# HGRN2's features split at once into the place of the padded values, and the recurrence's gated input formed on VectorE, in a two-layer hybrid decoder on one core

## The chip, the core and the metric

The kernel runs on one core of one Trainium2 chip, as one launch. The metric is device microseconds (us) of that core, and fewer is better. Times given as the time of a kernel are medians of several runs; the profile is one further execution, with its own time. The engines are TensorE (PE in the rows, with its weight loads as PEld), VectorE (DVE), ScalarE (ACT), GpSimd (POOL) and SyncE (SP), which issues the transfers.

## What is computed

The reference is a trunk of two layers over one sequence of 512 tokens with 1024 features, all in float32. Each layer adds a mixer and then a feed-forward block to x, and a last norm follows:

```
h = rmsnorm(x, norm1_w[l]);  proj = h @ w_in[l]
lx, lg, rq, rk, rv, rg, hq, hf, hi, hg = split(proj)
y_lru = rglru(lx, lg, ...)       # conv of 4 taps, gates r and i, a = exp(-8 r softplus(-lam)),
                                 # u = sqrt(1 - a*a) * (i * xc), scan h = a*h + u, times gelu(lg)
y_ret = retention(rq, rk, rv, rg, ...)   # rotary q and k, decaying scores, head norm, times silu(rg)
y_hg  = hgrn2(hq, hf, hi, hg, lb[l], ...) # S = diag(f) S + (1-f) v^T, o = S^T silu(q), head norm, times silu(hg)
x = x + concat(y_lru, y_ret, y_hg) @ w_out[l]
x = x + conv_ffn(rmsnorm(x, norm2_w[l]))  # up, conv of 3 taps, silu(gate) * val, down
```

Retention and HGRN2 have four heads of 64 features (256 each for q, k or f, v and the gate), the recurrence (RG-LRU) has 512 features. The lower bounds `lb` come from a softmax over the layers of a small parameter.

## The kernel before, in words

Features lie on partitions, tokens along the free dimension: x is eight tiles of 128 x 512. To keep float32 precision with quick matmuls, every operand is split into two fp32r parts, a high one made by a copy on ScalarE and a low one made by a subtraction on VectorE (`xh`, `xl` of x or y, `wh`, `wl` of a weight, `gh`, `gl` of the feed-forward block). A product is then three matmuls (`mm3`, lines 320 to 324): high by high (L321), high by low (L322), low by high (L323). A norm's factor is not multiplied into x: x is scaled by the norm's weight when it is split, and the factor `rb` of each token is applied when a projection leaves PSUM.

Weights arrive in pieces of 128 x 1024 through three raw buffers, are split two pieces ahead of their use (`split_w`, `next_w`, lines 291 to 318) and lie in four pairs of buffers. PSUM's eight banks are four for large products (`mm`) and four for small ones (`sm`).

The order of every engine's instructions is written out at build time. `Flow` (lines 77 to 154) is a small planner: each chain of work is a generator, TensorE's main stream advances a clock by a fixed cost per product, and whenever the clock passes a chain's due time that chain emits its next operations. So each engine has one fixed queue, in the order in which the planner emitted them, and an instruction that waits holds up everything behind it on its engine. All operations of VectorE, ScalarE and GpSimd go through one helper, so that they all stand under line 185 in the rows, and small matmuls under line 327.

**The start** (`main` and `begin`, lines 1289 to 1373). ScalarE issues the load of the first norm's weights; SyncE loads x and the first two weight pieces in turn, in pieces of 256 KB. Nine warming matmuls run meanwhile. ScalarE and VectorE split x0, then half a weight piece in two steps, and so on. The first two output tiles share each piece of x (`joint`, line 499). The squares of x and their sum `ssq` come after all splits. `finish_norm` (line 419) takes the two first norms (one of each layer) through four small matmuls to `rms_ps`, a Newton iteration on 128 x 4 numbers, and four more matmuls that spread the factor to `rms_rps`; the second norms use `rsqrt_wide` (line 358), two wide matmuls with a matrix of ones and then Ln, Exp and Square on ScalarE. `setup_lb` (line 480) makes the lower bounds some 27 us into the run:

```
484  V.tensor_tensor(out=mx, in0=p0, in1=p1, op=ALU.max)
486  V.tensor_tensor(out=ex[:, 0, :], in0=p0, in1=mx, op=ALU.subtract)
487  V.tensor_tensor(out=ex[:, 1, :], in0=p1, in1=mx, op=ALU.subtract)
488  A.activation(out=ex, in_=ex, func=AF.Exp)
489  V.tensor_tensor(out=mx, in0=ex[:, 0, :], in1=ex[:, 1, :], op=ALU.add)
490  V.reciprocal(out=mx, in_=mx)
```

and seven more on VectorE up to line 497. `setup_small` (line 449) makes the constants `lamc` of the recurrence, with small operations on VectorE.

**The projections** (`mixers`, lines 1042 to 1067) take 28 tiles' worth of products in this order: hf0 hq0 hf1 hq1, hv, rq0 rk0, rv, rq1 rk1, lx0 to lx3, hg0 hg1 rg0 rg1, lg0 to lg3. A tile is eight products of 512 columns. The values hv and rv are wanted with tokens on partitions, so x is the stationary operand there and the weight moves, 256 columns at a time:

```
1049  banks.append(mm_ps.tile([128, 2, 256], F32, name="vps", tag="mm"))
...
1057  mm3(banks[c // 2][:, c % 2, :], n.h[kk][:, ts], n.lo[kk][:, ts], wh[:, sl], wl[:, sl],
1058      hf == 0 and k == 0 and c % 2 == 0, hf == 1 and k == 3 and c % 2 == 1, cost=0.374)
```

Four token blocks by eight pieces of x make 32 products for hv and 32 for rv. `evac_v` (line 555) applies the factor of each token on ScalarE. `hg_values` (line 704) copies hv into `vz`, a padded form in which each half of the tokens has zeros for the other.

Beside the main stream run the chains: HGRN2's (`hg_forget`, `hg_query`, then `hg_chain` with seven levels, each a group of small matmuls into one `sm` bank and a copy out of it), the two rotary and retention chains, and the recurrence (`lru_conv`, `lru_batch`, `lru_gate`). In `lru_batch` (line 899) GpSimd forms the gated input: `G.tensor_tensor(out=gts[j][1], in0=gts[j][1], in1=xcs[j], op=ALU.mult)`. GpSimd also makes the silu products of the gates (line 625).

Finished features are split into two parts by `split_y` (line 608) for W_out, in the order HGRN2, retention, recurrence (tiles 6, 7, 4, 5, 0 to 3). They take the places of `xh0`, `xl0` and so on, so each waits until the last projection has used that piece of x (`xfree`). W_out (`ops`) begins with two output tiles of six products each and then the missing two of each. The feed-forward block (`pps` for up, `dps` for down) follows; the last down projection of layer 0 adds to x (`add_x`), splits the new x for layer 1 and sums its squares, there on GpSimd (`square_x`, line 402). Layer 1 then starts with two tiles that use six pieces of x before they need the last two.

Of the kernel before, what the change touches and what calls it, by code (L numbers as in the profile page):

```python
# [15 lines left out]
S = 512  # L16
# [12 lines left out]


FIRST = ["x0", 0, "x1", 1, "x2", "x3", 2, "x4", "x5", 3, "x6", "x7"]
# [13 lines left out]
PL = _o  # L45
# [3 lines left out]
for _n, _w in (  # L49
# [9 lines left out]
WCOL = {"lx": 0, "lg": 512, "hg": 2816, "rg": 1792}  # L59
TAIL = "lx0 lx1 lx2 lx3 hg0 hg1 rg0 rg1 lg0 lg1 lg2 lg3".split()  # L60
TAIL = [(t[:2], int(t[2])) for t in TAIL]

WIN = (
    [("f", 2304), ("f", 2048), ("f", 2432), ("f", 2176), ("v", 2560, 0), ("v", 2560, 1)]
    + [("f", 1024), ("f", 1280), ("v", 1536, 0), ("v", 1536, 1), ("f", 1152), ("f", 1408)]
    + [("f", WCOL[n] + 128 * j) for n, j in TAIL]
)
WNAMES = (
    [("hf", 0), ("hq", 0), ("hf", 1), ("hq", 1), "hv", None]
    + [("rq", 0), ("rk", 0), "rv", None, ("rq", 1), ("rk", 1)]  # L70
    + TAIL
)
# [136 lines left out]
def kernel(ctx, tc, x_in, win, wout, wup, wdn, lruw, params, consts, out):  # L209
# [4 lines left out]
    low.tile([128, 896], F32, name="spare")  # L214
# [17 lines left out]
    csm = const.tile([128, CSMALL], F32, name="csm")  # L232
    cbig = const.tile([128, 2 * S], F32, name="cbig")
    msk = const.tile([128, len(LEVELS) - 1, 32], U8, name="msk")
    lamc = const.tile([128, DEPTH, 4, 3], F32, name="lamc")
    lbc = const.tile([128, DEPTH, 2, 2], F32, name="lbc")

    const.tile([128, 32], F32, name="pad")
    rpool.tile([128, 32], F32, name="pad")
# [22 lines left out]
    for l in range(DEPTH):  # L262
        wlist += [win[l, i] for i in range(len(WIN))]
# [94 lines left out]
    def rsqrt_wide(sq, r, tile_of, weights, name):  # L358


        h, lo = tile_of(F32R, 0), tile_of(F32R, 1)
        A.activation(out=h, in_=sq, func=AF.Copy)
        yield None
        V.tensor_tensor(out=lo, in0=sq, in1=h.bitcast(F32), op=ALU.subtract)
        yield None
        ps = yield from psum([128, S], name)
        small(0.216, out=ps, lhsT=weights, rhs=h, start=True, stop=False)
        small(0.216, out=ps, lhsT=weights, rhs=lo, start=False, stop=True)
# [16 lines left out]
    def new_norm(nw, pool):  # L385
        n = Norm()
        n.pool = pool
        n.nw, n.h, n.lo, n.sq, n.rb = nw, {}, {}, 0, None
        n.ssq = None
        n.fast = n.wide = False  # L390
        return n
# [27 lines left out]
    def finish_norm(n):  # L419
        if n.wide:  # L420

            v = rpool.tile([128, S], F32, name="rb")
            yield from rsqrt_wide(n.ssq, v, lambda t, i: rpool.tile([128, S], t, name="sq", bufs=3), ones, "rms_ps")
            n.rb = v
# [1078 lines left out]
```

## Time and profile before

| what | us |
|---|---|
| median of 3 runs | 1169.06 (1168.43 to 1169.92) |
| profiled execution, its own time | 1168.12 |
| its span, first to last instruction | 1166.3 |
| TensorE busy | 1154.9 (99%) |
| VectorE busy | 781.1 (67%) |
| ScalarE busy | 534.3 (46%) |
| GpSimd busy | 64.9 (6%) |
| layer 0: projections, from 5.25 on | to 176.9 |
| layer 0: W_out | 176.9 to 221.0 |
| layer 0: feed-forward | 221.0 to 580.5 |
| layer 1: projections | 580.5 to 750.3 |

Matmuls are pipelined: a matmul's row gives a duration longer than its share of TensorE, so a busy TensorE isn't one at its peak, and the distance between two starts is the better measure. A time in brackets behind a row is the idle time of that engine just before, and what ended it. A row with "x4" is four instructions merged.

### The profile page before, as it was taken

The page shows a single profiled execution, that of the slowest core. Times are in us where ns is not written, and L with a number is a line of the kernel's source. Part 1 is how long each engine was busy: PE and PEld are TensorE (multiplying, and loading weights), DVE is VectorE, ACT ScalarE, POOL GpSimd, SP SyncE. Part 2 cuts the span into 40 slices and gives each one's busy share as a digit, 9 for nine tenths or more (in the row PEclk, how much of TensorE's full clock was granted, in tenths as well). Part 3 has the DMA queues.
Part 4 walks back from the last instruction along what each step waited for, and adds up shares of the span by engine and source line. Part 5 has one row for each costly group of instructions (what it writes and reads, how often), then busy time and mean ns, then how long its engine had stood idle before and what let it go on. Part 6 is the DMA issues. An engine that isn't in the chain of part 4 may idle for free.

```text
span 1166.3 us, 15226 instructions
## 1 busy us (share of the span) xinstructions
PE 1154.9 (99%) x6046; PEld 961.6 (82%) x6046; DVE 781.1 (67%) x1162; ACT 534.3 (46%) x722; POOL 64.9 (6%) x51
## 2 busy tenths in 40 slices
PE   9999999999999999999999999999999999999997
PEld 7888778888888888888888877888888888888886
DVE  7887887577774575474668486955876646745645
ACT  6536874464443343232542568545444424433422
POOL 1011210000000000000310012100000000000001
PEclk9999999999999999999999999999999999999999
DMA  7232223223323332322432221423232232233222
GB/s 257 94 99 56 72 73 125 92 90 106 93 76 105 109 87 89 113 86 76 126 103 81 73 82 37 140 88 98 91 99 96 80 121 93 76 105 104 82 71 88
DMA packets 36455, 111.79 MB, mean 96 GB/s; under 512 B 4512, under 2 KB 5024, under 8 KB 36384
## 3 DMA queue, kind: packets, MB, share of 16 engines
q1 hardware_dynamic: 34560, 108.59, 29.6%
q10 hardware_dynamic: 1824, 2.23, 0.7%
q8 instruction: 47, 0.77, 0.3%
q14 instruction: 24, 0.20, 0.0%
HBM read 106.61 MB, written 2.10 MB: 93 GB/s over the span
## 4 chain that ended last, share of the span: by engine, by line
PE 96%; DVE 2%; DMA 1%; issue 0%; SPq 0%; ACT 0%; POOLq 0%; POOL 0%; DVEq 0%
PE pps L321 20%; PE pps L323 19%; PE pps L322 19%; PE dps L322 7%; PE dps L321 7%; PE dps L323 7%; PE ops L322 3%; PE ops L321 2%; PE ops L323 2%; PE vps L321 1%; PE vps L322 1%; PE vps L323 1%; PE k_o L327 1%; PE hg_pl L327 1%; PE lr_ps L327 1%; DVE qp L185 1%
## 5 line engine op out<-in xcount | busy, mean ns | idle before, releaser
L321 PE MATMUL pps<-xh,wh 128*128 128x512 f32 x1024 | 403.5, 394 | 0.0
L323 PE MATMUL pps<-xh,wl 128*128 128x512 f32 x1024 | 399.4, 390 | 1.3 <-DVE wl L185 1.3
L322 PE MATMUL pps<-xl,wh 128*128 128x512 f32 x1024 | 398.9, 390 | 0.0
L185 ACT ACTIVATE wh<-raw 128x1024 fp32r<-128x1024 f32 (+3 forms) x211 | 204.8, 973 | 150.5 <-PE dps L322 103.3
L185 DVE TENSOR_TENSOR wl<-raw,wh 128x1024 fp32r<-128x1024 f32 (+3 forms) x211 | 243.2, 1155 | 12.8 <-ACT wh L185 12.8
L321 PEld LDWEIGHTS pps<-xh,wh 128*128 128x128 f32 x1024 | 192.5, 188 | 43.2 <-issue 3.5
L323 PEld LDWEIGHTS pps<-xh,wl 128*128 128x128 f32 x1024 | 192.3, 188 | 42.5 <-DVE wl L185 2.1
L322 PEld LDWEIGHTS pps<-xl,wh 128*128 128x128 f32 x1024 | 192.6, 188 | 39.0 <-DVE xl L185 0.4
L185 DVE SCALAR_TENSOR_TENSOR hs<-pps,rb 128x512 f32<-128x512 f32 x88 | 60.4, 690 | 129.6 <-PE pps L323 129.6
L321 PE MATMUL dps<-gh,wh 128*128 128x512 f32 x320 | 124.5, 389 | 0.0
L322 PE MATMUL dps<-gl,wh 128*128 128x512 f32 x320 | 124.5, 389 | 0.0
L323 PE MATMUL dps<-gh,wl 128*128 128x512 f32 x320 | 124.5, 389 | 0.0
L185 DVE TENSOR_TENSOR x<-x,dps 128x512 f32<-128x512 f32 (+1 forms) x72 | 44.9, 627 | 107.4 <-PE dps L323 107.0
L185 ACT ACTIVATE cg<-hs,prm 128x512 f32<-128x512 f32 x44 | 35.9, 816 | 85.1 <-DVE hs L185 85.1
L185 ACT ACTIVATE cg<-cg 128x512 f32<-128x512 f32 x44 | 27.8, 632 | 93.9 <-DVE cg L185 93.9
L321 PEld LDWEIGHTS dps<-gh,wh 128*128 128x128 f32 x320 | 60.1, 188 | 12.6
L323 PEld LDWEIGHTS dps<-gh,wl 128*128 128x128 f32 x320 | 60.1, 188 | 12.4
L322 PEld LDWEIGHTS dps<-gl,wh 128*128 128x128 f32 x320 | 60.1, 188 | 12.4
L185 DVE SCALAR_TENSOR_TENSOR cvv<-hs,prm,cvv 128x511 f32<-128x511 f32 x88 | 65.9, 748 | 1.8
L185 DVE SCALAR_TENSOR_TENSOR cg<-hs,prm,cg 128x511 f32<-128x511 f32 x88 | 65.7, 747 | 1.5
L185 ACT ACTIVATE gh<-cvv 128x512 fp32r<-128x512 f32 x44 | 27.8, 631 | 73.6 <-DVE cvv L185 73.6
L322 PE MATMUL ops<-xl,wh 128*128 128x512 f32 x128 | 50.1, 391 | 0.0
(218 smaller groups left out, 1275.1 us busy)
## 6 DMA issues: line engine op xcount, KB each, us to landing
raw<-in_wup_dram SPq DMA_DIRECT2D x88, 512.0 KB, 3.5
raw<-in_win_dram SPq DMA_DIRECT2D x46, 512.0 KB, 3.5
raw<-in_wdn_dram SPq DMA_DIRECT2D x48, 384.0 KB, 3.0
raw<-in_wout_dram SPq DMA_DIRECT2D x16, 512.0 KB, 3.5
raw<-in_wdn_dram SPq DMA_DIRECT2D x16, 256.0 KB, 2.6
x<-in_x_dram SPq DMA_DIRECT2D x8, 256.0 KB, 5.3
sw<-ev ACTq DMA_DIRECT2D x32, 64.0 KB, 2.1
raw<-in_win_dram SPq DMA_DIRECT2D x4, 256.0 KB, 5.0
```

Source lines behind the costliest of these rows:

```text
L185: return fn(*args, **kw)
L321: T.matmul(out=ps, lhsT=ah, rhs=bh, start=start, stop=False)
L322: T.matmul(out=ps, lhsT=ah, rhs=bl, start=False, stop=False)
L323: T.matmul(out=ps, lhsT=al, rhs=bh, start=False, stop=stop)
L327: T.matmul(**kw)
```

## The change

The four HGRN2 tiles hf0, hf1, hq0, hq1 become one block in both layers: each piece of x meets all four before the next one, for six pieces, and each tile then takes its last two. hv and rv become one block of 32 products with 512 columns, two of its token blocks in `sm` banks. The values are no longer scaled: the token's factor goes into the keys instead, for HGRN2 by a product with three operands on VectorE, for retention by a squared factor. Both first norms use the wide form; the one of layer 0 (`whole`) as one plain fp32 matmul. `split_y` puts HGRN2's two features into the place of `vz` without a wait, and moves the other six two places forward. The recurrence's gated input moves from GpSimd to VectorE. At the start, x and weights alternate piece by piece, the weights are split 512 columns at a time, the squares are taken among the splits, and the lower bounds (`setup_lb`, with one more operation per layer) are made right behind the split of x0, from two small loads of their own on ScalarE's queue. `setup_small` runs for both layers at once, five operations on VectorE and the rest on GpSimd. The sums of squares for layer 1 move to VectorE. Leading blanks are shortened here.

```diff
+JOINT = [("hf", 0), ("hf", 1), ("hq", 0), ("hq", 1)]
+ALONE = "rq0 rk0 rq1 rk1 lx0 lx1 lx2 lx3 hg0 hg1 rg0 rg1 lg0 lg1 lg2 lg3".split()
...
-    small(0.216, out=ps, lhsT=weights, rhs=lo, start=False, stop=True)
+    if tile_of is None:
+        ps = yield from psum([128, S], name)
+        small(0.9, out=ps, lhsT=weights.bitcast(F32), rhs=sq)
...
+    v = rpool.tile([128, S], F32, name="rb")
+    parts = None if n.whole else lambda t, i: rpool.tile([128, S], t, name="sq", bufs=3)
+    yield from rsqrt_wide(n.ssq, v, parts, ones, "rms_ps")
+    n.rb = v
...
+        V.tensor_scalar(out=lbc[:, l, :, 2], in0=lbc[:, l, :, 0], scalar1=0.5, scalar2=-0.5,
+                        op0=ALU.mult, op1=ALU.add)
+    setup_done.add("lb")
+def joint_tiles(n, done):
+    ws, pss = [], []
+    order = [(k, p) for k in range(KD - 2) for p in range(4)] + [(k, p) for p in range(4) for k in (KD - 2, KD - 1)]
+    for k, p in order:
+        if k // 2 == len(ws):
+            w = yield from next_w()
+            ws.append(w)
+        if k == 0:
+            yield from mm.take()
+            pss.append(mm_ps.tile([128, S], F32, name="pps", tag="mm"))
+        if k not in n.lo:
+            yield lambda: k in n.lo
+        wh, wl = ws[k // 2]
+        o = k % 2 * 512 + p * 128
+        mm3(pss[p], wh[:, o:o + 128], wl[:, o:o + 128], n.h[k], n.lo[k], k == 0, k == KD - 1)
+        yield None
+        if k == KD - 1:
+            done(p, pss[p])
...
+    if key[0] == "rk" and not rb2:
+        rb2.append(low.tile([128, NC, 2, 64], F32, name="hc_x").rearrange("p c h n -> p (c h n)"))
+        A.activation(out=rb2[0], in_=n.rb, func=AF.Square, scale=0.5)
+        yield None
-    V.tensor_tensor(out=t, in0=ps_of.pop(key), in1=n.rb, op=ALU.mult)
+    if key[0] == "rk":
+        V.tensor_tensor(out=t, in0=ps_of.pop(key), in1=rb2[0], op=ALU.mult)
+    else:
+        V.scalar_tensor_tensor(out=t, in0=ps_of.pop(key), scalar=-0.5, in1=n.rb, op0=ALU.mult, op1=ALU.mult)
...
-def evac_v(key):
...
+def values():
+    vz = low.tile([128, NC, 2, 256], F32, name="vz")
+    for b in range(2):
+        G.memset(vz[64 - 64 * b:128 - 64 * b, :, b, :], 0.0)
+    v = mp.tile([128, NC, 512], F32, name="v")
+    for c in range(NC):
+        yield has_ps(("v", c))
+        A.activation(out=v[:, c, :], in_=ps_of.pop(("v", c)), func=AF.Copy)
+        drop(sm if c < 2 else mm)
+    for b in range(2):
+        bs = slice(64 * b, 64 * b + 64)
+        A.activation(out=vz[bs, :, b, :], in_=v[bs, :, 0:256], func=AF.Copy)
+    vv["h"], vv["r"], vv["z"] = v[:, :, 0:256], v[:, :, 256:512], vz
+    yield None
+    evt.add("hv")
+    evt.add("rv")
...
 def split_y(src, k):
     i = YORDER.index(k)
-    yield has(("xfree", i))
-    h = xwpool.tile([128, S], F32R, name=f"xh{i}")
-    lo = xwpool.tile([128, S], F32R, name=f"xl{i}")
+    if i < 2:
+        if not ys:
+            ys.append(low.tile([128, 4, S], F32R, name="vz"))
+        h, lo = ys[0][:, 2 * i, :], ys[0][:, 2 * i + 1, :]
+    else:
+        yield has(("xfree", i - 2))
+        h = xwpool.tile([128, S], F32R, name=f"xh{i - 2}")
+        lo = xwpool.tile([128, S], F32R, name=f"xl{i - 2}")
...
-    V.tensor_scalar(out=kt, in0=kt, scalar1=olb, scalar2=None, op0=ALU.mult)
+    V.scalar_tensor_tensor(out=kt, in0=kt, scalar=lbc[:, l, ft, 2:3], in1=n.rb, op0=ALU.mult, op1=ALU.mult)
...
-        G.tensor_tensor(out=gts[j][1], in0=gts[j][1], in1=xcs[j], op=ALU.mult)
+        yield None
+        V.tensor_tensor(out=gts[j][1], in0=gts[j][1], in1=xcs[j], op=ALU.mult)
...
+yield from joint_tiles(n, done)
+banks, ws = [], []
+for q, c in [(q, c) for h in range(2) for q in range(2) for c in (2 * h, 2 * h + 1)] + [
+        (q, c) for q in (2, 3) for c in range(NC)]:
+    if q == len(ws):
+        w = yield from next_w()
+        ws.append(w)
+    wh, wl = ws[q]
+    ts = slice(c * 128, (c + 1) * 128)
+    if q == 0:
+        sl, pool, tag = ((sm, sm_ps, "sm") if c < 2 else (mm, mm_ps, "mm"))
+        yield from sl.take()
+        banks.append(pool.tile([128, 512], F32, name="vps", tag=tag))
+    for k in (2 * q, 2 * q + 1):
+        sl = slice(k % 2 * 512, k % 2 * 512 + 512)
+        mm3(banks[c], n.h[k][:, ts], n.lo[k][:, ts], wh[:, sl], wl[:, sl], k == 0, k == KD - 1)
+        yield None
+    if q == 3:
+        ps_of["v", c] = banks[c]
...
+    for l in range(DEPTH):
+        o = l * PL + PCOLS["lb"]
+        nc.scalar.dma_start(out=lbp[:, l, :], in_=params[:, o:o + 2])
+    for i in range(3):
         raws[i] = rawp.tile([128, 1024], F32, name="raw")
...
+    def piece(k):
+        c = slice(k % 2 * 512, k % 2 * 512 + 512)
+        nc.sync.dma_start(out=raws[k // 2][:, c], in_=wlist[k // 2][:, c])
+        fl.load(128 * 4 * 512)
+    for k in range(KD):
+        nc.sync.dma_start(out=x[k], in_=x_in[:, k, :])
         fl.load(128 * 4 * S)
+        if k < 6:
+            piece(k)
...
+        for k in range(6):
+            tile_x(k)
+            if k == 0:
+                setup_lb()
+            tile_w(k)
+            if k == 1:
+                raws[3] = rawp.tile([128, 1024], F32, name="raw")
+                piece(6)
+                piece(7)
+                nc.sync.dma_start(out=csm, in_=consts[:, 0:CSMALL])
+                fl.load(128 * 4 * CSMALL)
+                nc.sync.dma_start(out=prm[:, 8:], in_=params[:, 8:])
+                fl.load(128 * 4 * (DEPTH * PL))
+            if k in (3, 5):
+                fetch()
+            if k > 1:
+                square(k - 2)
+        for k in (6, 7):
+            tile_x(k)
+            square(k - 2)
+        square(6)
+        last = square_x(n, 7)
+        next(last)
+        next(last)
+        tile_w(6)
+        tile_w(7)
+        fetch()
...
-        setup_lb()
-        V.tensor_copy(out=ones, in_=dmean.to_broadcast([128, 128]))
...
+        n.fast = True
```

## Rows read from the trace of the kernel before

**Rows 1.** page, part 4: the chain that ended last, by engine
```profile
PE 96%; DVE 2%; DMA 1%; issue 0%; SPq 0%; ACT 0%; POOLq 0%; POOL 0%; DVEq 0%
```

**Rows 2.** waits of TensorE: line waited for: us in total, times, longest
```profile
PE pps L323 <- DVE wl L185: 1.3, 2, 0.6
```

**Rows 3.** busy time by stretch, 200 to 560 us: length, busy, count, clock, DMA
```profile
200.00:560.00 360.00, 360.00 (x1590) 1.00 0.31 93
```

**Rows 4.** timeline of TensorE, 31 to 33 us: start, duration, engine, line, operation
```profile
30.95 0.28 PE L321 MATMUL vps<-wh,xh 128*128 128x256 f32 x1
...
32.98 0.28 PE L323 MATMUL vps<-wh,xl 128*128 128x256 f32 x1
```

**Rows 5.** timeline of TensorE around the first norm of layer 0
```profile
21.33 1.05 PE L327 MATMUL rms_ps<-csm,ssq 128*128 128x1 f32 x8 [0.57 <-DVE ssq L185]
22.25 0.48 PE L321 MATMUL pps<-xh,wh 128*128 128x512 f32 x1
...
25.86 1.16 PE L327 MATMUL rms_rps<-csm,rms_rc 128*128 128x128 f32 x8
26.77 0.48 PE L321 MATMUL pps<-xh,wh 128*128 128x512 f32 x1
```

**Rows 6.** timeline of ScalarE and VectorE at the start
```profile
4.17 0.72 ACT L185 ACTIVATE xh<-x,prm 128x512 fp32r<-128x512 f32 x1 [1.49 <-DMA prm<-in_params_dram]
...
4.93 0.75 DVE L185 SCALAR_TENSOR_TENSOR xl<-x,prm,xh 128x512 fp32r<-128x512 f32 x1 [3.91 <-ACT xh L185]
...
7.24 0.69 DVE L185 TENSOR_TENSOR wl<-raw,wh 128x512 fp32r<-128x512 f32 x1 [0.23 <-ACT wh L185]
...
15.81 5.47 DVE L185 TENSOR_TENSOR ssq<-ssq,sq 128x512 f32<-128x512 f32 x7
```

**Rows 7.** timeline of TensorE at the start of W_out, layer 0
```profile
176.89 0.39 PE L321 MATMUL ops<-xh,wh 128*128 128x512 f32 x1
177.23 0.50 PE L322 MATMUL ops<-xl,wh 128*128 128x512 f32 x1
```

**Rows 8.** timeline of GpSimd: one of four gated inputs
```profile
124.43 1.30 POOL L185 TENSOR_TENSOR lr_g<-lr_g,qp 128x512 f32<-128x512 f32 x1 [8.77 <-ACT lr_g L185]
```

**Rows 9.** timeline of VectorE and GpSimd in the tail of layer 0
```profile
154.39 0.69 DVE L185 TENSOR_TENSOR ev<-pps,rb 128x512 f32<-128x512 f32 x1 [4.45 <-PE pps L323]
155.00 3.60 DVE L185 SCALAR_TENSOR_TENSOR qp<-qp,lr_g 128x512 f32<-128x512 f32 x4
158.52 3.45 DVE L185 TENSOR_TENSOR wl<-raw,wh 128x1024 fp32r<-128x1024 f32 x2
...
156.31 3.44 POOL L185 TENSOR_TENSOR ev<-ev,sq 128x512 f32<-128x512 f32 x2 [10.58 <-ACT sq L185]
```

**Rows 10.** timeline of VectorE: first and last of the set-up's twelve
```profile
26.86 0.15 DVE L185 TENSOR_TENSOR sm_m<-prm 128x2 f32<-128x2 f32 x1
...
28.87 0.17 DVE L185 TENSOR_SCALAR lbc<-lbc 128x2 f32<-128x2 f32 x1
```

**Rows 11.** timeline of TensorE at the start
```profile
1.06 4.21 PE L1301 MATMUL warm_ps<-zero 128*128 128x128 f32 x18 [1.06 <-DVE eps L1298]
...
6.33 0.63 PE L323 MATMUL pps<-xh,wl 128*128 128x512 f32 x1
6.75 0.57 PE L321 MATMUL pps<-xh,wh 128*128 128x512 f32 x1
7.15 0.39 PE L322 MATMUL pps<-xl,wh 128*128 128x512 f32 x1
7.38 0.39 PE L323 MATMUL pps<-xh,wl 128*128 128x512 f32 x1
```

**Rows 12.** timeline of VectorE: the copy out of a level's bank
```profile
48.56 1.30 DVE L185 COPY_PREDICATED st<-msk,hg_pl 128x512 f32<-128x512 uint8 x1
```

**Rows 13.** timeline of VectorE and TensorE where layer 1 starts
```profile
581.04 0.68 DVE L185 TENSOR_TENSOR x<-x,dps 128x512 f32<-128x512 f32 x1
...
582.54 0.39 PE L321 MATMUL pps<-xh,wh 128*128 128x512 f32 x1
```

More of the change, by code (lines that the diff above doesn't have):

```diff
@@ L213 @@
     const = ctx.enter_context(tc.tile_pool(name="const", bufs=1))
-    low.tile([128, 896], F32, name="spare")
+    low.tile([128, 864], F32, name="spare")
     xpool = ctx.enter_context(tc.tile_pool(name="xp", bufs=1))
@@ L262 @@
     for l in range(DEPTH):
-        wlist += [win[l, i] for i in range(len(WIN))]
+        wlist += [win[l, i] for i in range(NWIN)]
         wlist += [wout[l, m] for m in range(KD)]
@@ L389, in new_norm @@
         n.ssq = None
-        n.fast = n.wide = False
+        n.fast = n.whole = False
         return n
@@ L480, in setup_lb @@
+        G.tensor_tensor(out=s, in0=s, in1=z, op=ALU.mult)
+        G.tensor_scalar(out=s, in0=s, scalar1=2.0, scalar2=None, op0=ALU.mult)
+        G.tensor_tensor(out=s, in0=s, in1=rl, op=ALU.add)
+        for i, f in enumerate((-8.0, -16.0, 8.0)):
+            G.tensor_scalar(out=lamc[:, :, :, i], in0=s, scalar1=f, scalar2=None, op0=ALU.mult)
+        yield None
+    setup_done = set()
     def setup_lb():
         tp = rpool
-        p0, p1 = pc(0, "lb", 0, 2), pc(1, "lb", 0, 2)
+        p0, p1 = lbp[:, 0, :], lbp[:, 1, :]
@@ L1069, in mixers, with done @@
+        def done(i, ps):
+            ps_of[ALONE[i]] = ps
+        yield from matmul_tiles(n, len(ALONE), done, freed=lambda k: evt.add(("xfree", k)))
         n2 = new_norm(lambda k: pc(l, "n2", k), None)
-        n2.wide = True
         n2.fast = True
@@ L1298, in main @@
         nc.vector.memset(eps, EPS)
+        nc.vector.memset(mean, 1.0 / D)
+        nc.vector.tensor_copy(out=ones, in_=mean.to_broadcast([128, 128]))
         zps = sm_ps.tile([128, 128], F32, name="warm_ps", tag="sm")
@@ L1343, in begin @@
-            for i in range(2):
-                raws.pop(i)
-                ready[i] = ws[i]
-                fetch()
-            for _ in prep():
-                pass
-            for k in range(KD):
-                if k < KD - 1:
-                    for _ in square_x(n, k):
-                        pass
-                else:
-                    last = square_x(n, k)
-                    next(last)
-                    next(last)
-            fl.free.update(A=17.5, V=18.0)
-            fl.now = 5.8
@@ L1359, in begin, with tile_x @@
-            fl.spawn(last, 13.8)
+            ws = [(wp.tile([128, 1024], F32R, name="wh"), wp.tile([128, 1024], F32R, name="wl")) for _ in range(4)]
+            def tile_x(k):
+                h = xwpool.tile([128, S], F32R, name=f"xh{k}")
+                lo = xwpool.tile([128, S], F32R, name=f"xl{k}")
+                A.activation(out=h, in_=x[k], func=AF.Copy, scale=n.nw(k))
+                V.scalar_tensor_tensor(out=lo, in0=x[k], scalar=n.nw(k), in1=h.bitcast(F32),
+                                       op0=ALU.mult, op1=ALU.subtract)
+                n.h[k], n.lo[k] = h, lo
@@ L1360, in begin @@
+            for k in (6, 7):
[8 more added lines that the diff above has]
+            fetch()
+            fl.free.update(A=19.5, V=21.6)
+            fl.now = 5.2
+            fl.spawn(last, 15.0)
             yield 15.5
```

279 lines of the change are left out of this document (80 added, 199 removed).

## The prediction

> **What bounds the kernel.** I read the page first, its chain of work that ended last: 96% of it is TensorE [rows 1]. So a part of the change is worth what it takes out of TensorE's own stream of matmuls, plus the stalls that it removes, minus the stalls that it adds; time of another engine counts only where TensorE waits for it. The view of TensorE's waits says how little that is now: the longest entry is 1.3 us, in two waits [rows 2]. Because matmuls are pipelined, I price one by the distance from its start to the next start. In the quiet stretch from 200 to 560 us 1590 matmuls fill 360 us, 0.2264 us each [rows 3]; nearly all are 512 columns wide. A product (three matmuls) is therefore 0.68 us. The threshold used for the chances is 0.2% (2.3 us), about what a measurement of this kernel can tell from no change.
>
> **Values with 512 columns.** Before, hv and rv are 64 products of 256 columns in each layer, 384 matmuls in both. In a quiet piece 17 steps take 32.98 - 30.95 = 2.03 us, 0.1194 us each [rows 4]: 45.9 us. After, one block has 32 products of 512 columns in each layer, 192 matmuls at 0.2264: 43.5 us. That is -2.4 us. The small matmuls in between stay the same in number, and so do the changeovers between wide and small.
>
> **The two first norms.** Before, each takes two groups of eight passes: 22.25 - 21.33 = 0.92 us and 26.77 - 25.86 = 0.91 us [rows 5], 1.83 us a layer. In layer 1 they become two wide fp32r matmuls with the ones matrix, 0.45 us by [rows 3]: -1.4 us. In layer 0 it is one plain fp32 matmul of 512 columns, a form that this trace does not have. Bounds: 0.45 us (two such fp32r matmuls) and 0.92 us (eight fp32 passes of 128 columns [rows 5]); fp32 makes two passes here for each 128 columns, so I take the upper: -0.9 us. The first norm's matmuls also made TensorE wait 0.57 us for the sum of squares [rows 5]. After, the squares are done among the splits and the matmul stands 22 products into the stream instead of 21. What VectorE has to do by then, from 4.93 us on, is 14 splits of 0.69 to 0.75 us [rows 6], seven sums in 5.47 us [rows 6] and the set-up of 2.5 us worked out below; overlapping a little, that ends near 22 us, and the matmul comes at 23 us or later. That wait goes: -0.6 us. What is late next is rb, at about 29 us, as now; four tiles and eight products of the values run without it, to beyond 31 us, so nobody waits. ScalarE's added Ln, Exp and Square lie in that cover; beyond it every microsecond by which rb is later would cost one.
>
> **HGRN2's features split at once.** At the start of W_out the second matmul begins 0.34 us after the first instead of 0.23 [rows 7], because VectorE makes the low parts just in time. Two of eight splits leave this crowded place, and no copy waits for the last projection to let go of xh0: -0.3 us for both layers.
>
> **The gated input on VectorE.** GpSimd's product takes 1.30 us, four in each layer [rows 8]; VectorE needs 0.6 to 0.7 for one of that size [rows 9]. But VectorE is not free while GpSimd works: under the two products at 156.31 us, four operations of the size that takes 0.61 to the next start (154.39 to 155.00) take 3.60 us [rows 9], 1.2 us lost under the first of them, and the split behind them shows as much under the second. So VectorE gains or loses at most half a microsecond on each, in a stretch where TensorE has no wait. I cost it at nothing; what hides it is the two weights split ahead. In the same way the two-input product for kt in place of one-input, the squared rb for rk, lamc on GpSimd and the sums of squares of layer 1 moved from GpSimd to VectorE move work between engines that TensorE doesn't wait for. The 0.65 us stalls in each layer's tail [rows 2] come from GpSimd's silu products [rows 9], which stay; I leave them, bounds -1.3 and +1.3 us.
>
> **The start pays.** The change puts the whole set-up of the lower bounds between the split of x0 and that of the first weight. On VectorE and ScalarE it is a chain: three small operations, ScalarE's Exp, then nine more, from 26.86 to 29.04 us [rows 10], 2.2 us in the trace, and two multiplications are added (0.2 to 0.4): 2.5 us. Before, VectorE is through with xl0 at about 5.6 us and the third matmul, which needs the first low part of a weight, starts at 6.33 [rows 6, 11]. After, the set-up runs from 5.6 to 8.1, the first low part (now 512 columns, 0.69 us [rows 6]) is there at 8.8, and the third matmul starts there: +2.5 us. Nothing covers this; TensorE has nothing else to do. The small loads that the set-up needs follow the load of the norm weights, which lets ScalarE start at 4.17 us; issued 0.4 and 0.8 us behind it, they are there by about 5.2, before 5.6. From then on four tiles share each pair of x and weight, so 2.7 us of matmuls meet some 2.1 us of VectorE (two splits and a sum): no later hunger.
>
> Then the clock. The eighteen warming passes take 4.21 us, 0.23 each, against the 0.11 of such passes later [rows 5]; the first wide matmuls start 0.42 and 0.40 apart, and from 7.15 on 0.23 [rows 11]. The slow steps are the level of 1.2 GHz, the quick ones that of 2.4. Before the rise TensorE had worked from 1.06 us on with hardly a pause. After the change it pauses from 5.3 to about 7 and again from 7.8 to 8.8 us, and no row shows what the clock makes of that. Bounds: it is at the high level when work resumes (then the two slow steps go, -0.35 us), or as much low time lies behind the last pause as lay ahead of the rise in this trace, 6 us, to 14.8 us (14 matmuls, 12 more than before, at 0.2 us more each: +2.4 us). The row speaks for a late rise rather than none, so I take a value in the upper half: low to about 13 us, ten matmuls, eight more than before, +1.6 us. The Trainium skill, TensorE: Matmul & The Clock Gate, "What's actually happening", says that the low clock is the default and that activity releases it; the trace agrees with its two levels (0.42 and 0.23 us for the same matmul). By that rule the pauses speak against this change and the sum stands as it is; without it the sum would be about 2 us lower.
>
> **Sum:** -2.4 - 1.4 - 0.9 - 0.6 - 0.3 + 2.5 + 1.6 = -1.5 us. The profiled execution took 1168.12 us around a span of 1166.3, which gives 1166.6; the median of the runs is 1169.06, 0.94 above it, so the forecast for a median is **1167.5 us**.
>
> **Rivals.**
> A: the start does not pay twice. If the clock rises at once, or the set-up's small operations hide behind loads, the sum is between -3.4 (the clock alone) and -5.6 us (both), 1163.5 to 1165.7 us. For it: half of the set-up's time is the distance between tiny operations; against it: each waits for the one before, and the split of the weight stands behind them on both engines. Chance 0.27.
> B: slower, by the HGRN2 chain. Two of the four small PSUM banks now hold value products for some 22 us, just while the seven levels of the chain want a bank each. If the levels can no longer overlap the copy out of the bank before, each is late by such a copy, 1.30 us [rows 12], 8 us or more in all, and the recurrence behind it brings its features late to W_out. VectorE waits 4.45 us for TensorE ahead of the tail [rows 9], so there is about that much slack; the rival decides from 4.5 us of delay on, and at 8 us costs 3.5 us in each layer: 1167.5 + 7 = 1174.5 us. Against it: a level needs the keys and queries updated by the one before, so two banks should do. Chance 0.12.
> C: the beginning of layer 1. Four tiles now want four free banks at once. The last x sum starts at 581.04 us and lasts 0.68, and the fourth tile would start at 582.54 [rows 13], 0.8 us later. The sums of squares, now on VectorE, may use that up and 0.5 to 1.5 us more: 1168 to 1169 us, no change that can be told. Chance 0.13.
>
> **The numbers.** The forecast has 0.48. Around it lie the unknown tail (1.3 either way) and the clock's upper bound (0.8), 1166.2 to 1169.6 with both on one side. A gives faster; the forecast's own case lies close to the line at 1166.7 and gives 0.18 faster, 0.28 same and 0.02 slower; C gives same; B slower. Faster 0.45, same 0.41, slower 0.14. The range leaves out B and what lies beyond the other cases: 1163.0 to 1169.8.
>
> **What would show it.** Right: 192 value matmuls of 512 columns about 0.227 us apart; one rms_ps in layer 0 without a wait; a wait of some microseconds on wl before the third wide matmul, which starts near 8.8 us; steps of 0.42 us behind it. W_out of layer 0 then starts about 1 us from where it stands now, and layer 1 is 2 to 3 us shorter. Wrong: the third matmul before 7.5 us or quick steps at once (A); a gap on ops or pps ahead of the recurrence's features (B); a wait on x at the start of layer 1 (C).

## The result, and the profile after

The changed kernel takes **1175.73 us** (median of 4 runs, 1174.54 to 1177.04) beside 1168.74 us for the kernel before (4 runs, 1167.90 to 1169.92): a ratio of 1.0059, 95% interval 1.0043 to 1.0075. So it is slower, where the forecast was 1167.5 us and its range ended at 1169.8. The profiled execution took 1174.81 us around a span of 1173.0, 6.7 us over that of before.

The chain of work that ended last, by engine, in the page of the changed kernel (its part 4), which answers to [rows 1]:

```profile
PE 94%; DVE 4%; issue 1%; DMA 0%; POOL 0%; ACTq 0%; POOLq 0%; ACT 0%; DVEq 0%
```

VectorE now has 4% of the chain in place of 2%. The view of TensorE's waits (us in total, times, longest) says where, and answers to [rows 2]:

```profile
PE ops L313 <- DVE xl L175: 4.0, 4, 2.0
PE pps L312 <- ACT wh L175: 2.0, 1, 2.0
PE pps L314 <- DVE wl L175: 1.9, 2, 1.4
```

Two of these were forecast, the 2.0 us on ACT wh and 0.5 of the 1.9 on wl: the start. The others were not: 4.0 us in W_out on the low parts of the mixed features (three of the four waits in layer 0, the fourth, 0.63 us, in layer 1), and a stall of 1.4 us in layer 1's tail, that is in the last projections ahead of W_out. By stage, from the first to the first (or last) matmul of each, in the profiles of five kernels (the last three are explained below):

| stage, us | before | changed | product on GpSimd, own step (e5) | three edits (e7) | as e7, but product on VectorE (e10) |
|---|---|---|---|---|---|
| to the first matmul of W_out, layer 0 | 176.89 | 177.78 | 177.51 | 173.71 | 173.91 |
| W_out of layer 0, first to last | 43.85 | 49.82 | 46.11 | 44.63 | 48.95 |
| on to the first of layer 1 | 359.75 | 359.78 | 359.77 | 359.77 | 359.77 |
| on to W_out of layer 1 | 169.77 | 168.46 | 166.78 | 166.77 | 166.77 |
| W_out of layer 1, first to last | 43.29 | 44.21 | 43.29 | 43.29 | 44.13 |
| on to the last matmul | 365.73 | 365.75 | 365.75 | 365.76 | 366.12 |

So 0.9 us are lost up to W_out (forecast: about 1), **6.0 in W_out of layer 0**, and of layer 1's gain of some 3 us 1.7 are given back in its tail and 0.9 in its W_out.

**The start** came as forecast. TensorE of the changed kernel, against [rows 11] (start, duration, engine, line, operation, idle time ahead and its releaser):

```profile
7.21 0.79 PE L312 MATMUL pps<-xh,wh 128*128 128x512 f32 x1 [1.96 <-ACT wh L175]
...
8.95 0.80 PE L314 MATMUL pps<-xh,wl 128*128 128x512 f32 x1 [0.52 <-DVE wl L175]
9.54 0.63 PE L312 MATMUL pps<-xh,wh 128*128 128x512 f32 x1
9.97 0.63 PE L313 MATMUL pps<-xl,wh 128*128 128x512 f32 x1
...
13.38 0.48 PE L312 MATMUL pps<-xh,wh 128*128 128x512 f32 x1
```

The third matmul starts at 8.95 us instead of 6.33, and nine steps of 0.43 us follow, up to 13.4 us. Such a step, from one start to the next at the level of 1.2 GHz, is called a low step below; at the level of 2.4 GHz the step is 0.23 us. **Values** and the **first norm** of layer 0, against [rows 4, 5]:

```profile
26.44 1.02 PE L318 MATMUL rms_ps<-ssq,ones 128*128 128x512 f32 x2
26.90 0.80 PE L312 MATMUL pps<-xh,wh 128*128 128x512 f32 x1
27.54 0.40 PE L313 MATMUL pps<-xl,wh 128*128 128x512 f32 x1
...
33.47 0.39 PE L312 MATMUL vps<-wh,xh 128*128 128x512 f32 x1
...
37.10 0.39 PE L313 MATMUL vps<-wl,xh 128*128 128x512 f32 x1
```

Sixteen steps of the values take 3.63 us, 0.227 each. The norm is two passes without a wait. **W_out of layer 0**, against [rows 7]:

```profile
178.01 0.39 PE L313 MATMUL ops<-vz,wh 128*128 128x512 f32 x1
179.09 0.50 PE L314 MATMUL ops<-vz,wl 128*128 128x512 f32 x1 [0.69 <-DVE wl L175]
...
182.54 0.49 PE L313 MATMUL ops<-xl,wh 128*128 128x512 f32 x1 [2.02 <-DVE xl L175]
...
184.34 0.79 PE L313 MATMUL ops<-xl,wh 128*128 128x512 f32 x1 [0.84 <-DVE xl L175]
184.94 0.63 PE L314 MATMUL ops<-xh,wl 128*128 128x512 f32 x1
185.36 0.63 PE L312 MATMUL ops<-xh,wh 128*128 128x512 f32 x1
...
187.82 0.50 PE L313 MATMUL ops<-xl,wh 128*128 128x512 f32 x1 [0.55 <-DVE xl L175]
```

HGRN2's features are there (`vz` without a wait); what TensorE waits for, but for 0.69 us on a weight, is retention's and the recurrence's. The four waits are 4.1 us, and behind the third one come four low steps. That retention is late is seen on ScalarE, first the kernel before, then the changed one:

```profile
134.71 0.61 ACT L185 ACTIVATE sq<-rt_on 128x512 f32<-128x512 f32 x1
...
145.29 0.73 ACT L185 ACTIVATE lr_a<-lr_g,lamc 128x512 f32<-128x512 f32 x1
```

```profile
145.89 0.73 ACT L175 ACTIVATE lr_a<-lr_g,lamc 128x512 f32<-128x512 f32 x1
...
153.21 0.72 ACT L175 ACTIVATE lr_g<-lr_g,lamc 128x512 f32<-128x512 f32 x1
...
157.25 0.62 ACT L175 ACTIVATE sq<-rt_on 128x512 f32<-128x512 f32 x1
```

The Square with which the head norm of retention's second output begins stood 10.6 us ahead of the recurrence's batch (twelve Exp and Tanh); now it stands behind it, 22.5 us later than before. What hangs on it falls on VectorE into a stretch in which VectorE is hardly ever idle (changed kernel):

```profile
163.99 0.17 DVE L175 TENSOR_SCALAR hc_v<-hn_ps 128x8 f32<-128x8 f32 x1 [1.29 <-PE hn_ps L318]
...
165.41 1.21 DVE L175 SCALAR_TENSOR_TENSOR hc_nt<-hc_nt,hc_v 128x8 f32<-128x8 f32 x1
...
167.25 0.69 DVE L175 SCALAR_TENSOR_TENSOR hc_x<-hc_nt,hc_rc 128x512 f32<-128x512 f32 x1
...
181.80 0.69 DVE L175 TENSOR_TENSOR xl<-rt_on,xh 128x512 fp32r<-128x512 f32 x1
```

From 163.99 to the end of `hc_x` that is nearly 4 us, with 1.3 us of waiting ahead of it; the first scan of the recurrence starts at 172.60 us where it started at 166.23, and the splits that W_out waits for come behind that. The scans alone don't explain the waits: with the product on GpSimd (e5) the first scan starts at 172.92 us, and W_out is 3.7 us shorter all the same.

### The profile page after: what moved, and what is told of

It reads as the page before. It is cut to its first block, busy times and chain, and to the rows that moved or that the text cites. A ratio compares the mean times of both kernels' runs of the same rounds, so it can differ in the third digit from the quotient of the medians.

```text
span 1173.0 us, 14752 instructions
## 1 busy us (share of the span) xinstructions
PE 1154.7 (98%) x5826; PEld 949.2 (81%) x5826; DVE 777.2 (66%) x1113; ACT 543.9 (46%) x727; POOL 45.6 (4%) x59
## 4 chain that ended last, share of the span: by engine, by line
PE 94%; DVE 4%; issue 1%; DMA 0%; POOL 0%; ACTq 0%; POOLq 0%; ACT 0%; DVEq 0%
PE pps L312 19%; PE pps L314 19%; PE pps L313 19%; PE dps L312 7%; PE dps L314 7%; PE dps L313 7%; PE ops L313 2%; PE ops L314 2%; PE ops L312 2%; PE vps L312 1%; PE k_o L318 1%; PE hg_pl L318 1%; PE vps L314 1%; PE vps L313 1%; DVE wl L175 1%; DVE lr_g L175 1%
## 5 line engine op out<-in xcount | busy, mean ns | idle before, releaser
L175 ACT ACTIVATE wh<-raw 128x1024 fp32r<-128x1024 f32 (+2 forms) x212 | 204.8, 968 | 141.0 <-PE dps L313 103.3
L175 DVE TENSOR_TENSOR wl<-raw,wh 128x1024 fp32r<-128x1024 f32 (+2 forms) x212 | 239.3, 1132 | 20.3 <-ACT wh L175 20.3
L175 ACT ACTIVATE cvv<-hs,prm 128x512 f32<-128x512 f32 x44 | 35.9, 816 | 30.0 <-DVE hs L175 30.0
```

The source lines that it names most:

```text
L175: return fn(*args, **kw)
```

## Experiments

Theory: the loss is one of order, retention's second chain and the recurrence's batch changing places in queues that are fixed at build time. Rivals: the late start pushes everything; the early splits crowd VectorE; the product on VectorE costs its own time.

Runs of the kernel before beside them have medians of 1168.36 to 1168.70 us.

| run | edit (to the changed kernel, unless said) | median, us (runs) | ratio to before (95%) |
|---|---|---|---|
| e1 | set-up late | 1174.09 (4) | 1.0046 (1.0031 to 1.0061) |
| e2 | product on GpSimd, one step | 1171.36 (5) | 1.0035 (1.0020 to 1.0049) |
| e3 | HGRN2's split late | 1177.40 (4) | 1.0078 (1.0063 to 1.0093) |
| e4 | e1 and e2 | 1168.96 (10) | 1.0005 (0.9995 to 1.0014) |
| e5 | product on GpSimd, step of its own | 1168.70 (10) | 1.0004 (0.9995 to 1.0014) |
| e6 | Square first | 1171.69 (5) | 1.0033 (1.0020 to 1.0046) |
| e7 | e5, Square first, set-up late | **1163.18** (4) | **0.9957** (0.9942 to 0.9971) |
| e8 | kernel before, product on VectorE | 1169.21 (10) | 1.0008 (0.9999 to 1.0018) |
| e9 | Square first, set-up late, product on VectorE 2 us later | 1165.17 (6) | 0.9967 (0.9955 to 0.9980) |
| e10 | Square first, set-up late | 1168.85 (10) | 1.0002 (0.9993 to 1.0011) |
| e11 | 36 warming passes | 1175.36 (4) | 1.0053 (1.0038 to 1.0068) |
| e12 | e7 with HGRN2's split late | 1164.09 (4) | 0.9961 (0.9946 to 0.9975) |

### The start: e1 and e11

```
             for k in range(6):
                 tile_x(k)
-                if k == 0:
-                    setup_lb()
                 tile_w(k)
+                if k == 5:
+                    setup_lb()
```

Expected of e1: 

> Edit: the set-up of the lower bounds stands behind the sixth tile of x and weights (where it no longer precedes the first weight), nothing else moves. Order theory (the loss is in W_out of layer 0, made by the new order of the mixers' work): the start comes back to that of before (third wide matmul near 6.4 us instead of 8.95, low clock ending near 7 us instead of 13.4, four tiles done near 30.0), W_out of layer 0 still lasts about 50 us (50.05 now, 44.08 before), total 3.5 to 4.5 us under the changed kernel: 1171 to 1172 us. Rival (start theory: the late start and the late rb push every chain behind, and so the features): W_out of layer 0 falls back to 44 to 46 us as well, total 8 to 10 us under: 1165.5 to 1167.5 us.

Measured: the third matmul starts at 6.47 us, and W_out of layer 0 at 174.35, 3.43 us earlier. That is the start's price, and about the sum of its parts: 2.48 us of set-up and nine low steps at 0.2 us, less a wait of 0.95 us for the sum of squares that comes back. But W_out's four waits are the same to 0.02 us (0.68, 2.03, 0.82, 0.55), so the start theory falls. The median falls by 1.6 us only and misses the order theory's 1171 to 1172 us. In the profiled execution (1174.55 us) the clock took the rest: sixteen steps of 0.43 us in W_out instead of four. Two stretches of W_out, changed kernel and then e1 (length, busy time and count of PE, PEld, DVE, ACT and POOL, granted clock, DMA share, GB/s):

```profile
180.00:184.00 4.00, 1.48 (x6) 0.56 (x4) 4.00 (x7) 1.42 (x2) 0.00 (x0) 1.00 0.66 174
184.00:188.00 4.00, 3.11 (x7) 2.00 (x8) 4.00 (x6) 1.31 (x3) 0.00 (x0) 0.57 0.41 138
```

```profile
180.00:184.00 4.00, 3.01 (x7) 1.82 (x6) 4.00 (x6) 1.79 (x4) 0.00 (x0) 0.52 0.43 111
184.00:188.00 4.00, 3.62 (x9) 2.86 (x10) 2.22 (x4) 0.63 (x1) 0.00 (x0) 0.50 0.66 243
```

Only the quickest run of e1, 1171.80 us, lies in the order theory's range.

```
-WARM = 9
+WARM = 18
```

Expected of e11: 

> Edit to the changed kernel: thirty-six warming passes in place of eighteen (they multiply zeros and are read by nobody), so that TensorE works through the set-up of the lower bounds. Pause theory (TensorE's pauses of 2.0 and 0.5 us bring the low clock until 13.4 us): the third wide matmul still starts near 8.95 us, but its successors stand 0.227 us apart instead of 0.427 within a microsecond or so; nine steps of 0.2 us go, vps starts 1.5 to 2 us earlier (33.47 now), total 1173.5 to 1175 us. Rival (the clock rises at a time of its own whatever TensorE did): steps of 0.427 to 13.4 us as now, vps at 33.3 to 33.6.

```profile
1.05 7.23 PE L1312 MATMUL warm_ps<-zero 128*128 128x128 f32 x36 [1.05 <-DVE mean L1308]
...
8.87 0.50 PE L314 MATMUL pps<-xh,wl 128*128 128x512 f32 x1
9.20 0.40 PE L312 MATMUL pps<-xh,wh 128*128 128x512 f32 x1
9.44 0.39 PE L313 MATMUL pps<-xl,wh 128*128 128x512 f32 x1
```

With TensorE kept at work the third matmul stands where it stood, and from 9.20 us on the steps are 0.23 us. The values start at 31.22 us instead of 33.47. So the low clock at the start came of the pauses. The Trainium skill, TensorE: Matmul & The Clock Gate, "What's actually happening", has the low clock as the default that activity lifts; this pair of traces agrees. In the time it hardly shows (1175.36, just above the range expected): as in e1, sixteen low steps in W_out took back what the start gave.

### The product's engine: e2, e5, e8

```
-                yield None
-                V.tensor_tensor(out=gts[j][1], in0=gts[j][1], in1=xcs[j], op=ALU.mult)
+                G.tensor_tensor(out=gts[j][1], in0=gts[j][1], in1=xcs[j], op=ALU.mult)
```

Expected of e2: 

> Edit: the recurrence's gated input is formed on GpSimd again, in one step with the product before it; all else as changed. Order theory: W_out of layer 0 shrinks from 50.05 to 44 to 46 us, since the recurrence's batch and the second retention's chain stand as in the kernel before; total 4 to 6 us under the changed kernel, 1170 to 1172 us, the start as late as now (third matmul near 8.95 us). Start theory: the features are late all the same, 1174.5 to 1177 us.

In e5 the `yield None`, that is the step of its own, stays. Expected: 

> Edit: the recurrence's gated input on GpSimd, but in the step of its own that the change gave it. Engine theory (the product's place on VectorE makes the difference): as with GpSimd in one step, W_out of layer 0 lasts 45 to 47 us (49.82 in the changed kernel's profile, 46.23 with GpSimd in one step), total 1170 to 1172 us. Step theory (the extra step shifts the order of what is issued, whichever engine does the product): W_out 49 to 51 us, total 1174 to 1177 us.

In e8 it is the kernel before that gets `yield None` and `V.`. Expected: 

> Edit to the kernel before, not the changed one: only the recurrence's gated input goes to VectorE, in a step of its own. Order theory (the product on VectorE costs only where the new order of projections has put retention's second chain behind the recurrence): within 0.2% of the kernel before, 1167.5 to 1170 us, W_out of layer 0 at 44 to 45 us. Rival (the product on VectorE costs by itself, as four steps of 0.6 us in a full engine): W_out 46 to 48 us, 1171 to 1174 us.

Measured: with GpSimd W_out of layer 0 lasts 46.23 us (e2) and 46.11 (e5). e2 takes 1171.36 us, 4.4 under the changed kernel; it keeps a tail stall of 1.46 us in layer 1, with eight low steps behind it. e5 has none and takes 1168.70, below the range expected and **7.0 us under the changed kernel by this one product**. In W_out the engine theory holds against the step theory; in layer 1's tail the step counts too, since it is all that e2 and e5 differ in. In the old order (e8) the same move costs 0.8 us, just within what can be told from nothing; W_out lasts 45.03 us there, with one wait of 1.44, less than the rival wanted. So neither the product on VectorE nor the new order costs 7 us alone; together they do. TensorE's longest wait in W_out of e5:

```profile
PE ops L313 <- DVE xl L175: 2.2, 1, 2.2
```

In layer 1 the product's engine, in a step of its own, changes the order on ScalarE. Changed kernel and then e5:

```profile
719.30 0.72 ACT L175 ACTIVATE lr_a<-lr_g,lamc 128x512 f32<-128x512 f32 x1
...
727.25 0.62 ACT L175 ACTIVATE sq<-rt_on 128x512 f32<-128x512 f32 x1
```

```profile
715.69 0.63 ACT L175 ACTIVATE sq<-rt_on 128x512 f32<-128x512 f32 x1 [1.68 <-DVE rt_on L175]
...
717.64 0.72 ACT L175 ACTIVATE lr_a<-lr_g,lamc 128x512 f32<-128x512 f32 x1
```

Counted from layer 1's first matmul (587.38 and 583.40 us), the last Sigmoid ends at 129.01 us in both and retention's output leaves PSUM at 131.56 and 131.57. Only the queue differs: the planner has the batch issued ahead of the Square in one and behind it in the other. The batch needs nothing of the product; the quicker product merely lets the batch be issued 2.3 us sooner, and the Square then waits for all twelve. Layer 1 up to its W_out is 1.7 us longer for it (168.46 against 166.77 us, and 166.77 again in e6 below, where the Square is held ahead of the batch).

In layer 0, where e5 wins 3.7 us in W_out, this order does not change. In e2 and e5 the Square stands behind the batch as in the changed kernel: 2.5 us sooner in e5 (154.79 us), and only 0.25 us sooner in e2, whose W_out is just as short. ScalarE of e2:

```profile
145.63 0.72 ACT L175 ACTIVATE lr_a<-lr_g,lamc 128x512 f32<-128x512 f32 x1
...
157.00 0.61 ACT L175 ACTIVATE sq<-rt_on 128x512 f32<-128x512 f32 x1
```

What differs there comes behind the Square. These are the small matmuls that sum it on TensorE, in e2 and then in the changed kernel:

```profile
159.46 0.95 PE L318 MATMUL hn_ps<-csm,sq 128*128 128x2 f32 x8
```

```profile
163.00 0.95 PE L318 MATMUL hn_ps<-csm,sq 128*128 128x2 f32 x8
```

They stand 3.5 us later in TensorE's queue. `hc_x` then ends at 167.95 us instead of 164.69 in e2 (163.87 in e5), and retention's second low part, which W_out needs, at 184.29 instead of 181.53 (181.96 in e5). Which choice of the planner puts them later was not traced, and no run moves these matmuls alone. W_out of layer 1 does not follow the Square either: it lasts 43.32 us in e2, where the Square stands behind the batch (721.81 and 712.91 us), and 44.21 in the changed kernel.

### The split: e3 and e12

```
-            if i < 2:
...
-                h, lo = ys[0][:, 2 * i, :], ys[0][:, 2 * i + 1, :]
-            else:
...
-                yield has(("xfree", i - 2))
...
+            yield has(("xfree", i))
+            h = xwpool.tile([128, S], F32R, name=f"xh{i}")
+            lo = xwpool.tile([128, S], F32R, name=f"xl{i}")
```

Expected of e3: 

> Edit: HGRN2's mixed features wait again for the projections to let go of the x tiles; all else as changed. Order theory (the gate and the projections' order, not this split, make the features late): W_out of layer 0 stays at 50 to 51.5 us, and a wait on the first of HGRN2's features is added; total 0 to 2 us over the changed kernel, 1175.5 to 1178 us. Rival (crowding theory: the four early splits stand in VectorE's and ScalarE's fullest stretch ahead of the second retention's norm and push it back): W_out falls to 45 to 47 us, total 1171 to 1173 us.

Expected of e12: 

> Edit to the kernel with the three edits that took 1163.18 us: HGRN2's mixed features wait again for the projections to let go of the x tiles, as in the kernel before. If the split in the place of the padded values is worth what the forecast gave it (0.3 us for both layers), 1163 to 1164 us, with a wait of 0.1 to 0.5 us at the start of W_out; if it is worth what undoing it cost in the changed kernel (1.7 us), 1164.5 to 1165.5 us, with a wait of some 2 us there.

Measured: e3 takes 1177.40 us, W_out 50.41 with a wait of 3.74 us on the first of HGRN2's features: crowding falls, the early split is no part of the loss. e12 falls between its two expectations: the wait in W_out is 1.22 us instead of 0.68, W_out lasts 0.2 us longer (44.81), and the medians stand 0.9 us apart with intervals that overlap. So where the other features are in time the split is worth 0.2 to 0.9 us, which can't be told from the forecast's 0.3.

### Both first edits: e4

Expected: 

> Both of the first two edits: the set-up behind the sixth tile, and the gated input on GpSimd. Order theory: the two add up, 3.5 to 4.5 us from the start and 4 to 6 us from W_out of layer 0: 1166 to 1168 us, and below the kernel before. Start theory: as with the late set-up alone, 1165.5 to 1167.5 us, and no different from that one.

Measured 1168.96 us, 2.4 us under e2 alone and above the 1166 to 1168 expected. W_out starts at 174.39, as expected, and lasts 46.25; e2's stall in the tail of layer 1 is still there (1.46 us), and in the profiled execution, the slowest of the ten (1171.61 us), thirteen low steps follow it.

### The order alone: e6, e7, e9, e10

```
             sq = mp.tile([128, S], F32, name="sq", bufs=2)
             A.activation(out=sq, in_=src, func=AF.Square)
+            evt.add(("rsq", key))
...
             yield has(("on", ("h", 1)))
+            yield has(("rsq", ("r", 1)))
             for j in js:
                 r = gts[j][0]
```

Expected of e6: 

> Edit to the changed kernel: the recurrence's batch of twelve Exp and Tanh waits until the Square of retention's second output has been issued; the gate stays on VectorE. Late-norm theory (that Square stands behind the batch, at 157.25 us instead of 134.71, so its eleven small steps, 2.3 us, and their neighbours fall into the stretch in which VectorE is never idle, from 157 us on): the Square comes near 150 us, the small steps before 158, and although the batch is some 4 us later, TensorE's idle time in W_out of layer 0 falls from 4.1 us to 2 to 3, total 1172.5 to 1174.5 us. Rival (the recurrence's own chain is the bound): the batch is late by 4 us and W_out waits 4 us longer, total 1178 to 1180 us.

Measured 1171.69 us, **4.0 us under the changed kernel with the same operations on the same engines**. The Square stands at 149.78 us, the small steps end by 157, and the batch, 5.8 us later than in the changed kernel, harms less than expected: waits of 3.2 us in W_out, none in layer 1's tail. The total beat the expected range, the waits stayed above theirs. By stage the two profiles differ by 2.6 us: layer 1 up to its W_out is 1.7 us shorter and W_out of layer 0 1.2 (48.65), while 0.3 are lost at the start. W_out of layer 1 stays long (44.14).

Expected of e7 (e5's engine, e6's order, e1's set-up): 

> Three edits to the changed kernel: set-up behind the sixth tile, gated input on GpSimd in a step of its own, Square of retention's second output ahead of the recurrence's batch. If the losses are the start (3.4 us) and the features late at W_out of layer 0 (4.1 us of idle time and what the clock adds), both go: third wide matmul near 6.4 us, idle time in W_out at most 1 us, total 1164 to 1167 us, under the kernel before by 2 to 4 us. Rival (the loss moves to another wait, as in the tail of layer 1): 1168 to 1170 us.

```profile
PE ops L313 <- DVE xl L175: 0.7, 1, 0.7
PE rms_ps L318 <- DVE ssq L175: 0.7, 1, 0.7
```

Measured 1163.18 us, a little under the range expected and 5.2 us under the kernel before: it beats both. Its large products have no stretch of low steps.

In e9 the product stays on VectorE but is issued 2 us later; e10 is its control.

```
-                yield None
+                yield 2.0
                 V.tensor_tensor(out=gts[j][1], in0=gts[j][1], in1=xcs[j], op=ALU.mult)
```

Expected of e9: 

> Edits: set-up behind the sixth tile, Square of retention's second output ahead of the recurrence's batch, and the gated input on VectorE but issued 2 us later in the order, so that VectorE's queue need not stand on it until ScalarE's Sigmoid is through (1.58 us of idle time ahead of the third one in layer 0). Queue theory (VectorE may do the product for nothing if it is issued when its input is there): no idle time on VectorE ahead of lr_g, idle time of TensorE in W_out of layer 0 at most 1 us, total as with GpSimd, 1162.5 to 1164.5 us. Rival (four products of 0.6 us on VectorE cost by themselves): W_out idle 2 to 3 us, 1166 to 1168.5 us, as with the product issued at once.

Expected of e10: 

> The control for the run before: the same but for the 2 us, the product on VectorE issued at once. Queue theory: idle time of 1.5 us on VectorE ahead of the third lr_g in layer 0, TensorE's idle time in W_out of layer 0 about 3 us as with the Square first alone (3.16), total 3 to 4 us under that run's 1171.7: 1167.5 to 1169 us. Rival (with the start gone the place no longer matters): within 1 us of the run before.

Measured 1165.17 us, between the ranges of the two theories, and 1168.85, as expected: 3.7 us by the place of four products in a queue. But not for the reason given. VectorE's third product, in e9 and then in e10:

```profile
130.23 0.69 DVE L175 TENSOR_TENSOR lr_g<-lr_g,qp 128x512 f32<-128x512 f32 x1 [4.11 <-ACT lr_g L175]
```

```profile
130.87 0.69 DVE L175 TENSOR_TENSOR lr_g<-lr_g,qp 128x512 f32<-128x512 f32 x1 [1.58 <-ACT lr_g L175]
```

VectorE idles longer ahead of it in the better kernel, so that wait is not what counts, and the queue theory as I had put it falls. The difference shows in W_out, e9 and then e10:

```profile
176.97 0.69 DVE L175 TENSOR_TENSOR xl<-lr_g,xh 128x512 fp32r<-128x512 f32 x1
...
178.78 0.68 DVE L175 TENSOR_TENSOR xl<-lr_g,xh 128x512 fp32r<-128x512 f32 x1
179.38 2.35 DVE L175 TENSOR_TENSOR wl<-raw,wh 128x1024 fp32r<-128x1024 f32 x2
```

```profile
177.84 0.68 DVE L175 TENSOR_TENSOR xl<-lr_g,xh 128x512 fp32r<-128x512 f32 x1
178.45 2.35 DVE L175 TENSOR_TENSOR wl<-raw,wh 128x1024 fp32r<-128x1024 f32 x2
180.72 0.69 DVE L175 TENSOR_TENSOR xl<-lr_g,xh 128x512 fp32r<-128x512 f32 x1
```

In e9 two of the recurrence's low parts pass ahead of two weight splits (2.35 us), in e10 one does, and TensorE waits 1.91 us for the second, with low steps behind. Which chain the planner serves first there follows from the product's place 45 us earlier; the path from one to the other was not traced step by step. Between e9 and e7 2.0 us are left; how much of them is the four products' own time on VectorE, and how much is order, isn't shown.

e10 and e7 differ in the product's engine alone, with the Square ahead of the batch in both: **5.7 us** (1168.85 against 1163.18), by stage 4.3 in W_out of layer 0 and 0.8 in that of layer 1. So holding that one order leaves most of what the product's move costs.

## Why the prediction was wrong

**The step that failed is "The gated input on VectorE": "I cost it at nothing; what hides it is the two weights split ahead".** It weighed durations (0.7 us against 1.3, and the time that GpSimd's product takes from VectorE) and found them even. With the rest of the change held fixed the move costs 7.0 us (e5), and 5.7 with the set-up late and the Square held ahead of the batch (e10 against e7). Most of it lies in W_out of layer 0 (3.7 and 4.3 us). The operation's chain shares every queue with other chains, and its move changed places in them. In layer 1 the batch, which takes ScalarE for 8 us, passes ahead of retention's Square, 1.7 us. In W_out of layer 0 the low parts come later, without a change of place between Square and batch; there the same four products on the same engine, issued 2 us later, win back 3.6 us (e9 against e10). I named who waits for the product, not who is overtaken. By which choices of the planner the product's place reaches W_out some 45 us later stays open. "Values with 512 columns" failed beside it: it counted the matmuls and left out what the new order does to the other chains. With both value blocks ahead of retention's first query the query leaves PSUM at 68.87 us instead of 54.60, and retention's second output at 148.69 instead of 133.32, behind the start of the batch instead of ahead of it. That puts the Square behind the batch in layer 0, with the product on either engine; holding it ahead wins 4.0 us in the changed kernel (e6). No run changes the order of the projections alone, so its share, also in the 2.3 us that W_out of e5 still lasts longer than before, is argued from these rows and not shown.

**Most of the rest of the sum held.** Set-up +2.5: 2.48 (e1). Clock +1.6: nine low steps where the sum had ten; two stand there before, so seven are added, 1.4 us, and e11 shows that they go when the pauses are filled. Values -2.4: 192 matmuls at 0.227. Norms: layer 0's two fp32 passes take 0.46 us and the matmul behind them 0.64 instead of 0.23, 0.87 in all, near the upper bound (0.92) that I took for the kind of matmul; layer 1's stretch up to W_out is 3.0 us shorter in e5 and e7, 0.65 of it the old tail stall; the 2.35 left stand against 2.75 in the sum for that layer's values, norm and split. The wait for the sum of squares did go, but only under cover of the late start: without it 0.5 to 1.1 us of it are back (e1, e4, e7, e9). Split -0.3: 0.2 to 0.9 (e12). With the product on GpSimd the changed kernel takes 1168.70, 1.2 us from the forecast, and part of that nearness is luck: W_out of layer 0 is still 2.3 us longer than before, and the tail stalls that the sum had left alone, 1.3 us, are gone; with the start mended and the order held it takes 1163.18, and rival A's arithmetic for a start that costs nothing had given 1163.5.

**The rivals.** B gave 1174.5 us and named W_out as the place: right in sign and place, near in size by luck, and wrong in cause. HGRN2's two features are gated at 140.05 and 146.60 us, earlier than before (147.93 and 148.59), and the levels of its chain start 4.0 to 5.4 us apart, where they started 4.0 to 5.9 apart before; the price was worked out for the wrong chain. The tail stalls, left alone with bounds of 1.3 us either way, went in layer 0 and doubled to 1.38 us in layer 1, again by the Square's place: they are gone in e6. C did not come: no wait stands at the start of layer 1. A's case was refuted by the third matmul at 8.95 us.

## What to carry to other kernels

Where every engine's queue is written at build time, an operation moved to another engine is priced by what it lets pass: list the chains that meet on each engine around it, and see which margin between them is smaller than the shift. A margin that matters is better held by an explicit wait in the planner (here one line, the batch behind the Square, worth 4.0 us) than left to due times. But one order held doesn't hold the others: it left 5.7 us of the product's price. Parameters' set-up does not belong between the first operand and the first weight: it cost 2.5 us there, and nine low steps (1.8 us) stand behind it.

## What was not expected of the hardware

- A stall in TensorE's stream can cost more than its length, and not always the same. Behind the same four waits in W_out the profiles show four steps at the level of 1.2 GHz (changed kernel) or sixteen (e1, e11), 0.2 us each; behind a wait of 1.46 us in layer 1's tail eight (e2) or thirteen (e4), and behind one of 1.38 us (changed kernel) and one of 2.15 us (W_out of e5) none.
- The wide matmul that follows the two plain fp32 passes takes 0.64 us to the next start instead of 0.23 (26.90 to 27.54 above); the 0.41 us more are nearly as much as the passes themselves (0.46).
- A VectorE operation on 8 columns took 1.21 us instead of 0.17 (165.41 above) while GpSimd's product ran from 165.30 us for 1.29. The Trainium skill, SBUF — State Buffer, "SBUF: two separate sides", says that a VectorE instruction with two inputs in SBUF and a GpSimd instruction that reads SBUF exclude each other for the whole instruction; the trace agrees, down to this small operation. In e5 one with a single input waited as long (160.33 us, 1.21) while a GpSimd product ran from 160.21.
